# Feed-forward tiles laid out anew in SBUF, relu and square on ScalarE, Strassen-Winograd products in another order, last weights loaded in pairs

## The chip, the cores and the metric

The kernel runs on one core of a Trainium2 chip. Five engines work side by side, each on its own queue of instructions, in order: TensorE (PE, with its weight loads shown apart as PEld), VectorE (DVE), ScalarE (ACT), GpSimd (POOL) and SyncE (SP), which issues the DMAs here. Engines wait for each other on semaphores. The metric is the time of one execution on the device, in microseconds (us), as the median of the runs shown; less is better.

## The reference

One layer of a streaming encoder, for 512 prompt tokens and 64 sample tokens together (T = 576 columns), width 1024. Token mixing (a gated delta rule and a differential attention), a cross attention over a memory, and a feed-forward block, each added to the residual:

```python
h = x + concat([oa, ob]) @ w_out
h = h + mem_attn(rmsnorm(h, ln_mem_q), mem_k, mem_v, w_mem_q, w_mem_o)
hn = rmsnorm(h, ln_ffn)
h = h + square(relu(hn @ w_ff1)) @ w_ff2      # w_ff1 1024 x 4096, w_ff2 4096 x 1024
y = rmsnorm(h, ln_final)
```

All is float32. The change touches the feed-forward block and the step ahead of it.

## The kernel before

Activations lie transposed, features on the 128 partitions and tokens along the free axis, in blocks of 128 features (m = 0 to 7 for width 1024). A float32 product is made of three products of a rounded type (F32R): each operand is split into a high part, `A.copy` on ACT, and a low part, `V.tensor_tensor(... subtract)` on DVE, and PE adds high x high, high x low and low x high in PSUM.

**Order of the work.** The program is written in the order of the computation, and a planner makes from it the queue of each engine: among the instructions that it holds ready it takes the one that is earliest in the program, and `tc.high_priority()` raises what stands under it. A tile has a tag, and a tag has so many slots in its pool; an instruction that writes a new tile needs a free slot. At run time each queue is strictly in order, so an instruction that waits holds up all behind it on its engine, DMA issues on SP among them.

**Pools.** The stages up to the memory attention and `w_mem_o` use the pools `sp` (small tiles: B1, B0, kd, vb, p0, an, p1, X and so on, in this order of bytes) and `wp` (weights: `raw`, `wh`, `wl`). `work.close()` gives up both, and the pool `fp` of the feed-forward takes the same bytes, with waits tile by tile. Its tags lie in the order in which the program first names them: f1, rB, r1, s12, s34, a1h, a1l, w12h, w12l, a2h, a2l, w34h, w34l, keep, c, r2, w2h, w2l, tm.

**Ahead of the feed-forward.** For m in the order 0, 4, 1, 5, 2, 6, 3, 7, `project` multiplies with `w_mem_o`, `add_residual` adds to the residual `hT`, and `combine(m)` (L1220 to L1243) prepares the operands of a Strassen-Winograd product: the scaled activations are cut into upper and lower features (m < 4 or not) and first and second half of the tokens (N0, N1, 288 columns each), and the sums that the seven products need are split into B1, B2, T12 and T34. All sums are made in `combine(m)` for m of 4 and more. Then the squares are summed over the features by PE (`ones` and `accq`, bank `ba`), for the norm that is multiplied in later (rB).

**The first product.** `ff1_pair(p)` (L1281), p = 0 to 15, makes 256 of the 4096 hidden features. Two DMAs bring 512 KB of `w_ff1` each into r1 (two slots); DVE makes the weight sums s12 and s34 (L1293 to L1298), `split` makes a1, w12, a2 and w34 (L1270, L1271; one slot each). Then come seven products of 12 matmuls with 288 columns. Their sums stand in PSUM banks x (g0), y (gs), z (g1) and w (ba); `keep` copies a bank on ACT, `put` adds two parts on DVE (L1336), takes relu and square at once on DVE (L1337), and splits the result (L1341 on ACT, L1342 on DVE).

**The second product.** Groups of two pairs: with g = 1 to 7, the pairs 2g and 2g + 1 stand at m = 0 and m = 4, and for each m `weights2` brings 256 KB of `w_ff2` for group g - 1 into r2 (three slots), `project` multiplies, and `add_group` adds to the sum of the groups on DVE (L1372, L1374). Pairs 0 and 1 stand alone ahead, with `row_broadcast` (two ba banks) behind them. In the last group `last_weights` (L1380) brings the weights of group 7 for two m at each m of 4 and more, through r2, and splits them into the bytes of T34 and T12, which the last pair's products read. `last_block` then adds group 7 for each m, first half of the tokens, then second, and the final norm and the output follow.

PSUM has eight banks: pr (three), ba (two), g0, g1 and gs.

Of the kernel before, what the change touches and what calls it, by code (L numbers as in the profile page):

```python
# [37 lines left out]
def hybrid_layer_kernel(  # L38
# [1176 lines left out]
    T12, T34 = ([u[:, j].rearrange("p k (i t) -> p i k t", i=2) for j in range(2)] for u in (pair(2, F32R), pair(3, F32R)))  # L1215
    B1 = [cp.tile([P, 2, T], F32R, tag=f"qz{i}", name=nm("B1")).rearrange("p j (k t) -> p j k t", k=2) for i in range(2)]

    scaled = {}

    def combine(m):  # L1220


        scaled[m] = x = small("kd" if m < 4 else "aT", [P, T])
        A.activation(x, hT[m // 4][:, m % 4, :], AF.Identity, scale=gcol[:, G_FF + m : G_FF + m + 1])
        k = m % 4
        if m < 4:
            hi, lo = (B1[k // 2][:, j, k % 2, :] for j in range(2))
            A.copy(hi, x[:, N0])
            V.tensor_tensor(lo, x[:, N0], hi.bitcast(F32), ALU.subtract)
            return  # L1230
        top = scaled[k]
        t12, t34 = small("p0", [P, 2, NH]), small("an", [P, 2, NH])
        V.tensor_tensor(t12[:, 0], top[:, N1], top[:, N0], ALU.subtract)
        V.tensor_tensor(t34[:, 0], x[:, N1], top[:, N1], ALU.subtract)
        V.tensor_tensor(t12[:, 1], x[:, N1], t12[:, 0], ALU.subtract)
        V.tensor_tensor(t34[:, 1], x[:, N0], t12[:, 1], ALU.subtract)
        for (hi, lo), src in (
            ((T12[j][:, :, k, :] for j in range(2)), t12),
            ((B2[:, j, k, :] for j in range(2)), x),
            ((T34[j][:, :, k, :] for j in range(2)), t34),  # L1240
        ):
            A.copy(hi, src)
            V.tensor_tensor(lo, src, hi.bitcast(F32), ALU.subtract)  # L1243

    for m in (0, 4, 1, 5, 2, 6, 3, 7):
        project(weights(w_mem_o[0], m * P), mo, add_residual(m, True))
# [8 lines left out]
    work.close()  # L1255
    fp = ctx.enter_context(tc.tile_pool(name="fp", bufs=1, reuse_waits="tile"))

    def ft(tag, shape, bufs, dt=F32):
        return fp.tile(shape, dt, tag=tag, name=nm(tag), bufs=bufs)

    temps = lambda n: ft("tm", [P, 320], 2)[:, :n]
    odd = lambda: ft("f1", [P, 2, 4, T], 1, F32R)
    f1 = odd()
    rB = ft("rB", [P, T], 1)

# [15 lines left out]
    def ff1_pair(p, sx):  # L1281


        raw = []
        for i in range(2):
            raw.append(ft("r1", [P, 4, 2 * P], 2))
            src = w_ff1[0, 512 * i : 512 * i + 512, 2 * P * p : 2 * P * (p + 1)]
            nc.sync.dma_start(raw[i], src.rearrange("(k p) n -> p k n", p=P))
        A11, A21 = raw[0][:, :, :P], raw[0][:, :, P:]
        A12, A22 = raw[1][:, :, :P], raw[1][:, :, P:]  # L1290
        s12, s34 = (ft(tag, [P, 2, 4, P], 1) for tag in ("s12", "s34"))
        with tc.high_priority():
            V.tensor_tensor(s12[:, 0], A21, A22, ALU.add)  # L1293
            V.tensor_tensor(s12[:, 1], s12[:, 0], A11, ALU.subtract)
        a11, ws12 = split(A11, "a1", 1), split(s12, "w12", 1)
        with tc.high_priority():
            V.tensor_tensor(s34[:, 1], A12, s12[:, 1], ALU.subtract)
            V.tensor_tensor(s34[:, 0], A11, A21, ALU.subtract)  # L1298
        a2, ws34 = split(raw[1], "a2", 1), split(s34, "w34", 1)

        def block(w, c):
            return [x[:, :, c * P : (c + 1) * P] for x in w]

        def of(x, n):
            return lambda j, k: x[j][:, n, k, :]

        def half(u, n):
            return lambda j, k: u[:, j, k, n]

        operands = {  # L1310
            1: (a11, lambda j, k: B1[k // 2][:, j, k % 2, :]),
            2: (block(a2, 0), half(B2, N0)),
            3: ([x[:, 1] for x in ws34], half(B2, N1)),
            4: (block(a2, 1), of(T34, 1)),
            5: ([x[:, 0] for x in ws12], of(T12, 0)),
            6: ([x[:, 1] for x in ws12], of(T12, 1)),
            7: ([x[:, 0] for x in ws34], of(T34, 0)),
        }

        def product(i, b, start):  # L1320
            w, x = operands[i]
            for k in range(4):
                for j, (jw, jx) in enumerate(((0, 0), (0, 1), (1, 0))):
                    mm(
                        b[:, :NH], w[jw][:, k, :], x(jx, k),
                        start=start and k == j == 0, stop=k == 3 and j == 2, skip_group_check=True,
                    )

        def keep(b):
            x = ft("keep", [P, NH], 4)  # L1330
            A.copy(x, b[:, :NH])  # L1331
            return x

        def put(i, n, b, more):
            c = ft("c", [P, NH], 3)
            V.tensor_tensor(c, b, more, ALU.add)  # L1336
            V.scalar_tensor_tensor(c, c, 0.0, c, ALU.max, ALU.mult)  # L1337
            if p >= 2 * (NG - 1):
                V.tensor_tensor(c, c, rB[:, n], ALU.mult)
            hi, lo = (sx[:, j, 2 * (p % 2) + i, n] for j in range(2))  # L1340
            A.copy(hi, c)  # L1341
            V.tensor_tensor(lo, c, hi.bitcast(F32), ALU.subtract)  # L1342

        x, y, z, w = bank("g0"), bank("gs"), bank("g1"), bank("ba")
        product(1, x, True)
        s1 = keep(x)
        product(5, z, True)
        s5 = keep(z)
        product(2, y, True)
        put(0, N0, y[:, :NH], s1)  # L1350
        product(6, x, False)
        s2 = keep(x)
        product(3, z, False)
        put(0, N1, z[:, :NH], s2)
        product(7, x, False)
        s3 = keep(x)
        put(1, N1, s3, s5)
        product(4, w, True)
        put(1, N0, w[:, :NH], s3)

    accu = [None]

# [17 lines left out]
    def last_weights(m):  # L1380
        if m == 0:
            wlast.extend(pair(i, F32R) for i in (3, 2))
        hi, lo = (view(u, m // 4, 16, P)[:, 4 * (m % 4) : 4 * (m % 4) + 4] for u in wlast)
        raw = ft("r2", [P, 4, P], 3)
        nc.sync.dma_start(raw, w_ff2[0, (NG - 1) * 512 :, m * P : (m + 1) * P].rearrange("(k p) n -> p k n", p=P))
        A.copy(hi, raw)
        V.tensor_tensor(lo, raw, hi.bitcast(F32), ALU.subtract)

    def last_block(m, s, a0, n, alone=None):
        hi, lo = (view(u, m // 4, 16, P)[:, 4 * (m % 4) : 4 * (m % 4) + 4] for u in wlast)  # L1390
# [49 lines left out]
    for g in range(1, NG):  # L1440
        nxt = (f1 if g == 1 else odd()) if g % 2 else pair(5, F32R)
        for m in range(KT):
            if m % 4 == 0:
                ff1_pair(2 * g + m // 4, nxt)
            project(weights2(w_ff2[0, (g - 1) * 512 : g * 512, :], m * P), (pend,), add_group(g - 1, m), kt=4)
            if g == NG - 1:
                am, hm = accu[0][m // 4][:, m % 4, :], hT[m // 4][:, m % 4, :]
                V.tensor_tensor(am, am, rB, ALU.mult)
                V.tensor_tensor(hm, hm, am, ALU.add)
                if m >= 4:  # L1450
                    last_weights(2 * m - 8)
                    last_weights(2 * m - 7)
        pend = nxt
    pend = (pend,)

# [52 lines left out]
```

## Time and profile before

| | |
|---|---|
| median of 3 runs | 1036.83 us (1036.8 to 1037.14) |
| the profiled execution | 1037.32 us, its span 1035.6 us |
| PE busy | 1001.3 us, 97% of the span, 6630 matmuls |
| DVE, ACT busy | 733.2 us (71%), 488.5 us (47%) |
| DMA | 89.98 MB, mean 87 GB/s |
| mean granted PE clock | 0.991 |

The span is the time from the first to the last instruction of the profiled execution. Times in rows of the trace count from its start. A row of the timeline has the start, the duration, engine, line, operation, the output and input by the program's names, shapes and count, and in brackets how long the engine had been idle and what ended that. In tables of stretches a bracket holds the number of instructions. `SPq` is SP's queue; a wait `A <- B: total, times, longest` is time that A spent until B ended. All matmuls go through the helper in L107 and all transposes through L113, so tiles tell the stages apart.

### The profile page before, as it was taken

The numbers are of one execution on the slowest core, as the hardware profiler recorded it, in microseconds if no ns is written. First come the engines' busy times: TensorE is split into PE (matmuls) and PEld (weight loads), VectorE is DVE, ScalarE is ACT, GpSimd is POOL, SyncE is SP. The second block draws the span as 40 slices with busy tenths as digits, with TensorE's granted clock in tenths as the row PEclk, the third lists the DMA queues.
The fourth block names the chain that finished last, engine by engine and source line by source line (L and its number), as shares of the span: only waits on it lengthen the run. The fifth ranks groups of instructions, "written<-read, shape, count | busy, mean of one in ns | idle before, by whom it ended". The sixth has DMA issues, their size and how long they took to land.

```text
span 1035.6 us, 17242 instructions
## 1 busy us (share of the span) xinstructions
PE 1001.3 (97%) x6630; PEld 921.2 (89%) x6630; DVE 733.2 (71%) x1591; ACT 488.5 (47%) x1024; POOL 56.4 (5%) x123
## 2 busy tenths in 40 slices
PE   9999999999999999999999987999999999999986
PEld 7989899998888877999997986999999999999976
DVE  6576784776666676565665777966777777778883
ACT  6654664333465665444453554554333333343344
POOL 3431110100000000000000000000000000000000
PEclk9999999999999999999999997999999999999999
DMA  7432310100321455524111206232323232222122
GB/s 205 137 103 81 115 56 26 38 21 22 103 72 60 132 170 183 157 83 122 42 48 35 62 1 181 84 92 85 102 89 91 84 92 83 82 82 62 41 62 92
DMA packets 123365, 89.98 MB, mean 87 GB/s; under 512 B 5570, under 2 KB 114240, under 8 KB 122772
## 3 DMA queue, kind: packets, MB, share of 16 engines
q1 hardware_dynamic: 122916, 88.24, 28.7%
q8 instruction: 52, 0.85, 0.3%
q10 hardware_dynamic: 368, 0.66, 0.2%
q14 instruction: 29, 0.24, 0.1%
HBM read 79.14 MB, written 9.74 MB: 86 GB/s over the span
## 4 chain that ended last, share of the span: by engine, by line
PE 79%; DVE 6%; issue 3%; DMA 3%; ACT 3%; POOL 2%; POOLq 0%; ACTq 0%; SPq 0%; DVEq 0%
PE pr L107 46%; PE g L107 19%; PE gs L107 7%; DMA r<-in_w_ff_dram 3%; PE ba L113 2%; PE ba L107 2%; PE g L113 2%; DVE wl L162 0%; ACT w12h L1270 0%; DMA out_dram<-S 0%; POOL tg L208 0%; DVE p L457 0%; DVE a2l L1271 0%; DVE c L1336 0%; DVE c L1337 0%
## 5 line engine op out<-in xcount | busy, mean ns | idle before, releaser
L107 PE MATMUL pr<-u,wh 128*128 128x320 f32 (+2 forms) x1240 | 328.5, 342 | 1.8 <-DVE p L323 1.0
L107 PE MATMUL pr<-u,wl 128*128 128x256 f32 (+1 forms) x816 | 228.1, 303 | 0.0
L107 PEld LDWEIGHTS pr<-u,wh 128*128 128x128 f32 x1240 | 211.6, 188 | 18.1 <-DVE p L323 1.3
L107 PEld LDWEIGHTS pr<-u,wl 128*128 128x128 f32 x816 | 149.4, 188 | 3.8 <-issue 0.7
L162 DVE TENSOR_TENSOR wl<-raw,wh 128x1024 fp32r<-128x1024 f32 x65 | 79.5, 1224 | 36.6 <-ACT wh L161 36.1
L107 PE MATMUL pr<-u,w2h 128*128 128x320 f32 (+1 forms) x384 | 98.7, 340 | 5.5 <-ACT w2h L1270 3.8
L161 ACT CAST wh<-raw 128x1024 fp32r<-128x1024 f32 x65 | 68.2, 1049 | 60.5 <-PE pr L107 54.8
L1270 ACT CAST w2h<-r 128x512 fp32r<-128x512 f32 x56 | 34.7, 621 | 121.8 <-PE pr L107 102.6
L107 PE MATMUL pr<-f,w2h 128*128 128x320 f32 (+1 forms) x288 | 74.7, 340 | 0.3 <-DVE u L1374 0.2
L107 PEld LDWEIGHTS pr<-u,w2h 128*128 128x128 f32 x384 | 64.9, 188 | 10.9 <-ACT w2h L1270 4.4
L107 PE MATMUL pr<-u,w2l 128*128 128x256 f32 (+1 forms) x256 | 65.2, 295 | 0.0
L1372 DVE TENSOR_TENSOR u<-u,pr 128x256 f32<-128x256 f32 x96 | 42.2, 451 | 20.7 <-PE pr L107 20.5
L107 PEld LDWEIGHTS pr<-f,w2h 128*128 128x128 f32 x288 | 48.6, 188 | 4.1 <-issue 1.3
L107 PE MATMUL g<-u,w12h 128*128 128x288 f32 x256 | 52.2, 296 | 0.0
L107 PE MATMUL g<-u,w34h 128*128 128x288 f32 x256 | 51.7, 296 | 0.2 <-ACT keep L1331 0.2
L107 PE MATMUL pr<-f,w2l 128*128 128x256 f32 (+1 forms) x192 | 48.8, 294 | 0.0
L107 PEld LDWEIGHTS pr<-u,w2l 128*128 128x128 f32 x256 | 46.8, 188 | 1.5 <-DVE w2l L1271 0.2
L1271 DVE TENSOR_TENSOR w2l<-r,w2h 128x512 fp32r<-128x512 f32 x56 | 38.6, 690 | 8.4 <-ACT w2h L1270 8.3
L208 POOL TENSOR_TENSOR tiny<-tiny,nhalf 128x1 f32<-128x1 f32 (+4 forms) x10 | 8.3, 826 | 642.4 <-DVE tiny L1431 550.4
L107 PEld LDWEIGHTS g<-u,w12h 128*128 128x128 f32 x256 | 41.8, 189 | 0.5
L107 PEld LDWEIGHTS g<-u,w34h 128*128 128x128 f32 x256 | 41.0, 188 | 0.6 <-ACT keep L1331 0.6
L107 PE MATMUL pr<-wh,u 128*128 128x512 f32 x128 | 41.4, 402 | 0.0
(444 smaller groups left out, 2185.7 us busy)
## 6 DMA issues: line engine op xcount, KB each, us to landing
r<-in_w_ff_dram SPq DMA_DIRECT2D x32, 512.0 KB
r<-in_w_ff_dram SPq DMA_DIRECT2D x64, 256.0 KB
raw<-in_w_in_dram SPq DMA_DIRECT2D x28, 512.0 KB
raw<-in_w_mem_k_dram SPq DMA_DIRECT2D x8, 512.0 KB
raw<-in_w_mem_v_dram SPq DMA_DIRECT2D x8, 512.0 KB
raw<-in_w_out_dram SPq DMA_DIRECT2D x8, 512.0 KB
raw<-in_w_mem_q_dram SPq DMA_DIRECT2D x8, 512.0 KB
raw<-in_w_mem_o_dram SPq DMA_DIRECT2D x8, 512.0 KB
```

The costliest lines, as they stand in the source:

```text
L107: i = nc.tensor.matmul(out, lhsT, rhs, start=start, stop=stop, skip_group_check=skip_group_check)
L113: i = nc.tensor.transpose(out, in_, ident[:n, :n])
L161: A.copy(wh, raw)
L162: V.tensor_tensor(wl, raw, wh.bitcast(F32), ALU.subtract)
L208: G.tensor_tensor(out, in_, bc(nhalf[: in_.shape[0], 0:1], list(in_.shape)), ALU.pow)
L1270: A.copy(wh, src)
L1271: V.tensor_tensor(wl, src, wh.bitcast(F32), ALU.subtract)
L1372: V.tensor_tensor(am, am, b, ALU.add)
```

## The change

1. `fp` names its tags in another order, through a list of tiles made ahead of use (`laid`): r1 now has the first bytes, then keep, s12, r2, w2h, s34, a1h, a1l, w12h, w12l, a2h, a2l, w34h, rB, c, tm, w34l, f1, w2l. Sizes and numbers of slots stay.
2. `combine(m)` for m < 4 also makes the first T12 sum and its split; for m of 4 and more the second T12 sum is split alone, then B2, then T34.
3. In `put`, relu and square are two activations on ACT in place of one operation on DVE. The last `put` takes its sum straight from the bank, with no add on DVE.
4. The products come in the order 1, 5, 6, 2, 7, 3, 4 in place of 1, 5, 2, 6, 3, 7, 4. x is a ba bank in place of g0 and takes products 1, 6, 7 and 4 one upon the other; before, product 4 had a bank of its own.
5. `last_weights` loads two m with one DMA of 512 KB through r1, and splits them with one cast and one subtraction at high priority.

```diff
@@ combine
-    scaled = {}
+    scaled, steps = {}, {}
+
+    def halves_to(hi, lo, src):
+        A.copy(hi, src)
+        V.tensor_tensor(lo, src, hi.bitcast(F32), ALU.subtract)
...
         if m < 4:
-            hi, lo = (B1[k // 2][:, j, k % 2, :] for j in range(2))
-            A.copy(hi, x[:, N0])
-            V.tensor_tensor(lo, x[:, N0], hi.bitcast(F32), ALU.subtract)
+            halves_to(*(B1[k // 2][:, j, k % 2, :] for j in range(2)), x[:, N0])
+            steps[k] = t12 = small("p0", [P, 2, NH])
+            V.tensor_tensor(t12[:, 0], x[:, N1], x[:, N0], ALU.subtract)
+            halves_to(*(T12[j][:, 0, k, :] for j in range(2)), t12[:, 0])
             return
-        top = scaled[k]
-        t12, t34 = small("p0", [P, 2, NH]), small("an", [P, 2, NH])
-        V.tensor_tensor(t12[:, 0], top[:, N1], top[:, N0], ALU.subtract)
+        top, t12, t34 = scaled[k], steps[k], small("an", [P, 2, NH])
+        V.tensor_tensor(t12[:, 1], x[:, N1], t12[:, 0], ALU.subtract)
+        halves_to(*(T12[j][:, 1, k, :] for j in range(2)), t12[:, 1])
+        halves_to(*(B2[:, j, k, :] for j in range(2)), x)
         V.tensor_tensor(t34[:, 0], x[:, N1], top[:, N1], ALU.subtract)
-        V.tensor_tensor(t12[:, 1], x[:, N1], t12[:, 0], ALU.subtract)
         V.tensor_tensor(t34[:, 1], x[:, N0], t12[:, 1], ALU.subtract)
-        for (hi, lo), src in (
-            ((T12[j][:, :, k, :] for j in range(2)), t12),
-            ((B2[:, j, k, :] for j in range(2)), x),
-            ((T34[j][:, :, k, :] for j in range(2)), t34),
-        ):
-            A.copy(hi, src)
-            V.tensor_tensor(lo, src, hi.bitcast(F32), ALU.subtract)
+        halves_to(*(T34[j][:, :, k, :] for j in range(2)), t34)
@@ the pool fp
+    laid = {}
     def ft(tag, shape, bufs, dt=F32):
+        if tag in laid:
+            return laid.pop(tag)
         return fp.tile(shape, dt, tag=tag, name=nm(tag), bufs=bufs)
...
+    for tag, shape, bufs, dt in (
+        ("r1", [P, 4, 2 * P], 2, F32), ("keep", [P, NH], 4, F32), ("s12", wide_, 1, F32),
+        ("r2", block_, 3, F32), ("w2h", block_, 3, F32R), ("s34", wide_, 1, F32),
+        ("a1h", block_, 1, F32R), ("a1l", block_, 1, F32R), ("w12h", wide_, 1, F32R), ("w12l", wide_, 1, F32R),
+        ("a2h", [P, 4, 2 * P], 1, F32R), ("a2l", [P, 4, 2 * P], 1, F32R), ("w34h", wide_, 1, F32R),
+        ("rB", [P, T], 1, F32), ("c", [P, NH], 3, F32), ("tm", [P, 320], 2, F32), ("w34l", wide_, 1, F32R),
+        ("f1", [P, 2, 4, T], 1, F32R), ("w2l", block_, 3, F32R),
+    ):
+        laid[tag] = fp.tile(shape, dt, tag=tag, name=nm(tag), bufs=bufs)
@@ ff1_pair
         def put(i, n, b, more):
             c = ft("c", [P, NH], 3)
-            V.tensor_tensor(c, b, more, ALU.add)
-            V.scalar_tensor_tensor(c, c, 0.0, c, ALU.max, ALU.mult)
+            if more is None:
+                A.activation(c, b, AF.Relu)
+            else:
+                V.tensor_tensor(c, b, more, ALU.add)
+                A.activation(c, c, AF.Relu)
+            A.activation(c, c, AF.Square)
...
-        x, y, z, w = bank("g0"), bank("gs"), bank("g1"), bank("ba")
+        x, y, z = bank("ba"), bank("gs"), bank("g1")
         product(1, x, True)
         s1 = keep(x)
         product(5, z, True)
         s5 = keep(z)
+        product(6, x, False)
+        s2 = keep(x)
         product(2, y, True)
         put(0, N0, y[:, :NH], s1)
-        product(6, x, False)
-        s2 = keep(x)
+        product(7, x, False)
+        s3 = keep(x)
         product(3, z, False)
         put(0, N1, z[:, :NH], s2)
-        product(7, x, False)
-        s3 = keep(x)
         put(1, N1, s3, s5)
-        product(4, w, True)
-        put(1, N0, w[:, :NH], s3)
+        product(4, x, False)
+        put(1, N0, x[:, :NH], None)
@@ last_weights
-        hi, lo = (view(u, m // 4, 16, P)[:, 4 * (m % 4) : 4 * (m % 4) + 4] for u in wlast)
-        raw = ft("r2", [P, 4, P], 3)
-        nc.sync.dma_start(raw, w_ff2[0, (NG - 1) * 512 :, m * P : (m + 1) * P].rearrange("(k p) n -> p k n", p=P))
-        A.copy(hi, raw)
-        V.tensor_tensor(lo, raw, hi.bitcast(F32), ALU.subtract)
+        hi, lo = (
+            view(u, m // 4, 16, P)[:, 4 * (m % 4) : 4 * (m % 4) + 8].rearrange("p (i k) n -> p i k n", i=2) for u in wlast
+        )
+        raw = ft("r1", [P, 4, 2 * P], 2)
+        src = w_ff2[0, (NG - 1) * 512 :, m * P : (m + 2) * P]
+        nc.sync.dma_start(raw, src.rearrange("(k p) n -> p k n", p=P))
+        src = raw.rearrange("p k (i n) -> p i k n", i=2)
+        with tc.high_priority():
+            A.copy(hi, src)
+            V.tensor_tensor(lo, src, hi.bitcast(F32), ALU.subtract)
...
                     last_weights(2 * m - 8)
-                    last_weights(2 * m - 7)
```

More of the change, by code (lines that the diff above doesn't have):

```diff
@@ L1262, in hybrid_layer_kernel @@
     odd = lambda: ft("f1", [P, 2, 4, T], 1, F32R)
+    block_, wide_ = [P, 4, P], [P, 2, 4, P]
+    for tag, shape, bufs, dt in (
[7 more added lines that the diff above has]
+        laid[tag] = fp.tile(shape, dt, tag=tag, name=nm(tag), bufs=bufs)
     f1 = odd()
```

## The prediction

> **What bounds the kernel now.** I read the page's engine row and slices first, then the stretches around the two places where PE is not full, then the rows in time there, and last what SP waited for.
>
> ```profile
> PE 1001.3 (97%) x6630; PEld 921.2 (89%) x6630; DVE 733.2 (71%) x1591; ACT 488.5 (47%) x1024; POOL 56.4 (5%) x123
> PEclk9999999999999999999999997999999999999999
> ```
>
> PE bounds the program as a whole, so only idle PE time and slow PE clock can be won. One slice, two thirds in, has both. Stretches (columns: PE, PEld, DVE, ACT, POOL busy, granted clock, DMA share, GB/s):
>
> ```profile
> 616.00:618.00 2.00, 0.73 (x8) 0.65 (x7) 0.98 (x2) 1.36 (x3) 0.00 (x0) 1.00 0.00 0
> 618.00:622.00 4.00, 0.72 (x5) 0.63 (x4) 3.24 (x8) 1.79 (x3) 0.00 (x0) 0.51 0.00 0
> 622.00:626.70 4.70, 0.00 (x0) 0.00 (x0) 0.79 (x2) 0.60 (x1) 0.00 (x0) 0.50 0.71 222
> 626.70:631.60 4.90, 4.83 (x19) 4.61 (x20) 4.68 (x8) 3.99 (x7) 0.00 (x0) 0.50 0.87 233
> 640.50:643.00 2.50, 0.76 (x4) 0.41 (x4) 2.50 (x3) 2.49 (x4) 0.00 (x0) 1.00 0.79 240
> 643.00:654.60 11.60, 11.42 (x85) 11.19 (x86) 11.01 (x23) 5.47 (x12) 0.00 (x0) 1.00 0.29 92
> 654.60:985.00 330.40, 329.96 (x2265) 318.36 (x2264) 259.54 (x497) 128.80 (x241) 0.00 (x0) 1.00 0.28 82
> 985.00:996.60 11.60, 7.76 (x46) 6.63 (x45) 10.15 (x21) 3.72 (x6) 0.00 (x0) 1.00 0.47 136
> ```
>
> From 654.6 to 985 PE lacks 0.44 us: nothing done to DVE or ACT there can gain. The feed-forward's entry (616 to 643) and its end (985 to 996.6) remain. The entry in time, with what SP waited for:
>
> ```profile
> SPq L1288 <- DVE u L1243: 35.1, 1, 35.1
> ...
> 575.87 11.22 SPq L157 DMA_DIRECT2D raw<-in_w_mem_o_dram  x3
> 622.27 0.92 SPq L1288 DMA_DIRECT2D r<-in_w_ff_dram  x2
> ...
> 617.66 1.06 PE L107 MATMUL ba<-ones,accq 128*128 128x1 f32 x6 [1.27 <-DVE accq L1110]
> ...
> 620.73 0.67 ACT L1242 CAST u<-an 128x576 fp32r<-128x576 f32 x1 [0.37 <-DVE an L1236]
> ...
> 621.43 0.76 DVE L1243 TENSOR_TENSOR u<-an,u 128x576 fp32r<-128x576 f32 x1
> ...
> 626.10 0.62 ACT L1270 CAST a1h<-r 128x512 fp32r<-128x512 f32 x1 [4.70 <-DMA r<-in_w_ff_dram]
> 626.10 0.69 DVE L1298 TENSOR_TENSOR s<-r 128x512 f32<-128x512 f32 x1 [3.91 <-DMA r<-in_w_ff_dram]
> 626.75 0.69 DVE L1271 TENSOR_TENSOR a1l<-r,a1h 128x512 fp32r<-128x512 f32 x1
> 626.77 0.85 PE L107 MATMUL g<-B,a1h 128*128 128x288 f32 x2 [8.05 <-ACT a1h L1270]
> ```
>
> SP is done with w_mem_o's issues at 587.09, then stands 35.1 us before the first w_ff1 load, because that load's bytes lie under `an`, whose last reader (L1243) ends at 622.19. Data, cast and first product follow in series. PE also runs at half clock until 631.6.
>
> **The layout.** Counted from the shapes, the old pools' region begins with B1 and B0 (bytes 0 to 8,192 per partition); p0 lies at 16,896 to 22,016 and `an` at 22,016 to 27,136. Before, r1 lies at 20,736 to 28,928. After, r1 takes 0 to 8,192, whose last readers are the memory attention's products:
>
> ```profile
> L107 PEld LDWEIGHTS g<-an,B x8: 191/192/193, 547.9 to 571.4; 128*128 128x128 f32 x8
> ```
>
> So both w_ff1 loads of the first pair can go at 587 instead of 622.27 and are in long before they are wanted. The casts are another matter. In ACT's and DVE's queues of before, everything of the new pool stands behind the last combine (ACT 620.73, DVE 621.43, above), and I take it that this stays, since the planner lays out the new pool only when the old one's users are placed. The last combine itself shortens little: six DVE operations as before, one of them half as long. I take its end at 621.9 (0.3 earlier), a1h then runs from 621.4 to 622.0, and PE starts at 622.0 instead of 626.77: **gain 4.8**. Bounds: nothing, and 626.77 - 615.9 - 1.1 for the norm's products = 9.8 if the casts move ahead of the combine.
>
> The third matmul needs a1l. DVE runs L1298 and then a1l, 0.6 apart and 0.69 long: 623.2, which is 1.2 after the start where before it was 0.7: **loss 0.5**. The half clock lasted 4.9 us from the start; the idle stretch ahead of it shrinks from 8.1 to some 3.3 us, but the clock had fallen at 618 already. I leave it: 0 (bounds 0 and 2.4, half of 4.9). [...]
>
> **The second pair and SP's queue.** Before, PE stood 1.74 of the 2.5 us to 643 with the second pair's weights late:
>
> ```profile
> 630.84 5.08 DMA r<-in_w_ff_dram
> ...
> 636.04 0.69 DVE L1293 TENSOR_TENSOR s<-r,r 128x512 f32<-128x512 f32 x1 [1.79 <-DMA r<-in_w_ff_dram]
> ...
> 642.03 0.50 PE L107 MATMUL pr<-u,w2h 128*128 128x512 f32 x1 [1.50 <-DVE u L1342]
> ...
> 654.57 1.06 PE L107 MATMUL ba<-ident,tiny 128*128 128x128 f32 x8
> ```
>
> These loads wait for r1, so for the first pair's DVE work, which now starts 4.2 us earlier without waiting for data. The three w_ff2 loads that stand ahead of them on SP wait too: r2 now covers p0 and the first of `an`, so they go at about 620.5 to 622 instead of 623.2 to 625.3, and what is behind them is not held up further, as r1 comes free only at 624. DVE has less to do here as well (next part). Against it, product 4 had its own bank and filled PE while w12l was missing; now it adds to x behind product 7 and can't. I take **0.7 of the 1.74** (bounds -1 and 1.74). So the second pair ends at 654.57 - 5.0 = 649.6.
>
> **Relu and square.** Per pair four DVE operations of L1337 go, and one of the four adds of L1336 (put(1, N0) reads the finished sum from x); ACT gets four relus and four squares and loses one keep.
>
> ```profile
> L1337 DVE SCALAR_TENSOR_TENSOR c<-c 128x288 f32<-128x288 f32 x64 | 29.1, 456 | 1.0
> L1331 ACT COPY keep<-g 128x288 f32<-128x288 f32 x61 | 23.9, 392 | 6.8 <-PE g L107 6.8
> L1341 ACT CAST f<-c 128x288 fp32r<-128x288 f32 x32 | 13.8, 433 | 34.8 <-DVE c L1337 25.1 <-DVE c L1339 9.5
> L696 ACT ACT_TABLE_LOAD  x3: 1283/1283/1283, 125.8 to 186.1; - x3
> ```
>
> Over 16 pairs: DVE -64 x 0.456 - 16 x 0.456 = -36 us; ACT +128 x 0.392 to 0.433 - 16 x 0.392 = +44 to +49 us, and its idle time from 654.6 to 985 is 202 us. No trace has a Relu; a table load of 1.283 at each change would add 128 x 1.283 = 164 us to ACT and fill it. I take none: the run's last load is the one at 186.1, and Exp, Square, copies and casts alternate behind it. [...] In the stage itself DVE's relief is worth nothing.
>
> **The order 1 5 6 2 7 3 4.** Product 7 adds to x after keep(s2), product 4 after keep(s3), each with one product between. Before, only product 7 had so little room:
>
> ```profile
> 778.37 1.58 PE gs L107 x12
> ...
> 781.45 1.05 ACT L1270 CAST w12h<-s 128x1024 fp32r<-128x1024 f32 x1
> 782.41 0.39 ACT L1331 COPY keep<-g 128x288 f32<-128x288 f32 x1
> ...
> PE g L107 <- ACT keep L1331: 0.2, 1, 0.2
> ```
>
> A product gives 1.58 us; w12h and the keep behind it end 1.35 us after w12h's start. That fits, and cost 0.2 us in 16 pairs. After, relu, square and cast of a put share the window. I take **a loss of 0.6**; bounds 0 and one ACT operation of 0.4 at each of 32 places, 12.8.
>
> x also holds one of the two ba banks for a whole pair; the next pair takes the other. row_broadcast wants both once, between pairs; in the 0.6.
>
> **combine.** A T12 cast and its subtraction become two halves each, four times: ACT +4 x (2 x 0.43 - 0.67), DVE +4 x (2 x 0.46 - 0.76), 1.4 us together, spread under w_mem_o's products, where PE is full; if uncovered, those 1.4.
>
> **The end.** Before, the last weights shared r2's three slots with the stream that feeds PE:
>
> ```profile
> 984.43 0.37 SPq L1276 DMA_DIRECT2D r<-in_w_ff_dram  x1
> 986.76 1.60 SPq L1385 DMA_DIRECT2D r<-in_w_ff_dram  x2
> 988.76 0.37 SPq L1276 DMA_DIRECT2D r<-in_w_ff_dram  x1
> ...
> 987.39 0.62 ACT L1270 CAST w2h<-r 128x512 fp32r<-128x512 f32 x1 [3.30 <-DMA r<-in_w_ff_dram]
> ...
> 988.06 0.80 PE L107 MATMUL pr<-u,w2h 128*128 128x512 f32 x3 [2.82 <-ACT w2h L1270]
> 992.71 0.79 PE L107 MATMUL pr<-u,w2h 128*128 128x512 f32 x3 [1.01 <-ACT w2h L1270]
> ```
>
> After, four loads of 512 KB go to r1, idle once the last pair is split; two of them fit ahead of time. So PE's 2.82 + 1.01 = 3.83 us go. The splits become four of 1.05 on ACT and 1.22 on DVE instead of eight of 0.62 and 0.69, raised in priority, and must still wait for product 4, the last reader of those bytes. DVE is next: 10.15 of 11.6 us busy there, and PE's banks wait for its adds. I give back 0.8: **gain 3.0** (bounds 1 and 3.83).
>
> **Sum.** 4.8 - 0.5 + 0.7 - 0.6 + 3.0 = 7.4. The profiled execution took 1037.32 (span 1035.6 and 1.7 around it): 1029.9. The median of the runs is 0.5 lower, 1036.83: **1029.4**.
>
> **Rivals.**
> 1. The first pair's casts are placed ahead of the last combine. For: their data is there from 591 on (587.09 and the 3.8 us from issue to cast above), they are of high priority, and ACT has time. Against: the queue order above. Then PE starts right behind the norm and the half clock hardly bites: 9.8 + 2.4 + 0.7 - 0.6 + 3.0 = 15.3, so 1021.5.
> 2. The start is given back: the second pair's loads stay behind w_ff2's and PE waits for them as it did, or DVE, busy 11.01 of 11.6 us before 654.6, keeps the pace. 4.8 becomes 1: 1036.8 - 3.6 = 1033.2; with the end given back to DVE too, no change.
> 3. Slower: the keeps. Product 7 and 4 wait for a keep that stands behind a put's square and cast, 0.4 us, at 2 places in 16 pairs: 12.8 against 8.0 gained elsewhere: 1041.6. It decides from 0.25 us per place. For: room of only 0.23 us in the rows above. Against: PE's queue can hold w_ff2 products between, and DVE's lighter load brings puts sooner.
>
> **Chances.** Forecast 0.60 (1026 to 1033), first rival 0.14, second 0.13 (0.06 of it within 0.2%, which is 2.1 us and about what a measurement of this kernel tells from no change), third 0.13. So faster 0.81, same 0.06, slower 0.13. Range 1021 to 1037: it takes in the first two rivals and leaves out the third and the best of the first, under 2 in 10; the forecast's own is 1026 to 1033.
>
> **What would show it.** The first w_ff1 loads issued near 587; a1h right behind the last combine's cast with no wait for a DMA; PE's first product near 622 and the half clock still there; row_broadcast's products near 649.6; no wait for w2h after 985; keep waits of well under 1 us in all. Wrong would be: ACT table loads in the feed-forward, PE waiting for keep again and again, or a1h ahead of the last combine.

## The result, and the profile after

The changed kernel took 1035.14 us (median of 12 runs, 1033.1 to 1036.36), the kernel before 1037.08 us beside it (12 runs, 1035.79 to 1040.56): a ratio of 0.9975, 95% interval 0.9964 to 0.9985. That is 2.6 us gained (1.6 to 3.7) where 7.4 were forecast. The profiled execution took 1033.64 us, its span 1031.9 (before 1037.32 and 1035.6).

The entry of the feed-forward came out as drawn. First what SP issued and what PE, ACT and DVE did there (start, duration, idle before and its releaser):

```profile
586.73 1.12 SPq L1301 DMA_DIRECT2D r<-in_w_ff_dram  x2
620.49 2.40 SPq L1289 DMA_DIRECT2D r<-in_w_ff_dram  x3
...
620.44 0.67 ACT L1221 CAST u<-an 128x576 fp32r<-128x576 f32 x1 [1.34 <-DVE an L1241]
621.02 0.61 ACT L1283 CAST a1h<-r 128x512 fp32r<-128x512 f32 x1
...
621.69 0.85 PE L107 MATMUL ba<-B,a1h 128*128 128x288 f32 x2 [3.62 <-ACT a1h L1283]
623.16 0.61 PE L107 MATMUL ba<-B,a1l 128*128 128x288 f32 x1 [0.63 <-DVE a1l L1284]
636.62 0.53 PE L107 MATMUL ba<-u,a2h 128*128 128x288 f32 x2 [1.00 <-ACT keep L1344]
...
649.92 0.60 PE L107 MATMUL ba<-ident,tiny 128*128 128x128 f32 x4
```

The first w_ff1 loads go at 586.73 instead of 622.27, the a1h cast stands directly behind the last combine's cast with no DMA to wait for, and PE starts at 621.69 instead of 626.77. `row_broadcast`'s products behind the second pair stand at 649.92 (forecast 649.6).

The stretches (columns as in the prediction: PE, PEld, DVE, ACT, POOL busy, granted clock, DMA share, GB/s; the number in brackets counts instructions) show where the rest is missing. The kernel before:

```profile
600.00:660.00 60.00, 48.77 (x326) 46.84 (x326) 46.95 (x87) 29.56 (x52) 0.00 (x0) 0.89 0.31 92
660.00:972.00 312.00, 311.56 (x2134) 300.38 (x2133) 243.31 (x464) 120.53 (x223) 0.00 (x0) 1.00 0.29 85
972.00:1000.00 28.00, 24.16 (x157) 22.24 (x156) 24.47 (x50) 9.27 (x18) 0.00 (x0) 1.00 0.23 66
```

The changed kernel:

```profile
600.00:660.00 60.00, 53.45 (x354) 50.70 (x353) 46.86 (x84) 37.60 (x74) 0.00 (x0) 0.91 0.28 82
660.00:972.00 312.00, 310.47 (x2129) 298.99 (x2128) 213.72 (x394) 156.66 (x327) 0.00 (x0) 1.00 0.29 86
972.00:1000.00 28.00, 24.09 (x151) 21.91 (x151) 23.66 (x47) 12.24 (x25) 0.00 (x0) 1.00 0.12 38
```

At the entry PE is busy 4.68 us more. In the middle stage it is busy 1.09 us less, although DVE was relieved of 29.6 us. At the end PE lacks 3.91 us of 28, as before (3.84). The reason for the last is in PE's and DVE's rows of the changed kernel:

```profile
981.67 0.55 PE L107 MATMUL pr<-u,w2h 128*128 128x320 f32 x2 [1.70 <-DVE u L1389]
987.29 0.54 PE L107 MATMUL pr<-u,w2h 128*128 128x320 f32 x2 [2.21 <-DVE u L1391]
...
976.82 2.36 DVE L1409 TENSOR_TENSOR u<-r,u 128x1024 fp32r<-128x1024 f32 x2 [0.45 <-ACT u L1408]
980.80 0.81 DVE L1389 TENSOR_TENSOR u<-u,pr 128x256 f32<-128x256 f32 x2
982.72 1.22 DVE L1409 TENSOR_TENSOR u<-r,u 128x1024 fp32r<-128x1024 f32 x1
984.92 1.23 DVE L1409 TENSOR_TENSOR u<-r,u 128x1024 fp32r<-128x1024 f32 x1 [0.30 <-ACT u L1408]
986.73 0.42 DVE L1391 TENSOR_TENSOR u<-u,pr 128x256 f32<-128x256 f32 x1
```

PE no longer waits for w2h. It waits 1.70 + 2.21 = 3.91 us for the additions of `add_group` (L1389, L1391) that empty its pr banks, and on DVE these stand behind the big subtractions of the last weights (L1409), which the change raised in priority; between the first two of those and L1389 four smaller operations, 1.7 us in all, stand as well. One wait was exchanged for another of the same size.

### The profile page after: what moved, and what is told of

Its sections match the earlier page's. It is cut to its first block, busy times and chain, and to the rows that moved or that the text cites. A ratio compares the mean times of both kernels' runs of the same rounds, so it can differ in the third digit from the quotient of the medians.

```text
span 1031.9 us, 17262 instructions
## 1 busy us (share of the span) xinstructions
PE 1001.4 (97%) x6630; PEld 920.4 (89%) x6630; DVE 701.0 (68%) x1511; ACT 534.9 (52%) x1152; POOL 56.8 (6%) x123
## 4 chain that ended last, share of the span: by engine, by line
PE 77%; DVE 8%; DMA 4%; issue 3%; ACT 3%; POOL 2%; POOLq 0%; ACTq 0%; DVEq 0%; SPq 0%
PE pr L107 42%; PE g L107 14%; PE ba L107 9%; PE gs L107 8%; DMA r<-in_w_ff_dram 3%; PE ba L113 2%; PE g L113 2%; DVE w34l L1284 1%; DVE a2l L1284 1%; ACT w34h L1283 1%; DVE s L1307 1%; DVE s L1306 0%; DVE w2l L1284 0%; DVE wl L162 0%; DVE s L1310 0%
## 5 line engine op out<-in xcount | busy, mean ns | idle before, releaser
L1389 DVE TENSOR_TENSOR u<-u,pr 128x256 f32<-128x256 f32 x96 | 40.5, 451 | 10.6 <-PE pr L107 10.2
L1284 DVE TENSOR_TENSOR w12l<-s,w12h 128x1024 fp32r<-128x1024 f32 x16 | 19.6, 1225 | 35.7 <-ACT w12h L1283 35.7
L107 PEld LDWEIGHTS pr<-f,w2l 128*128 128x128 f32 x192 | 35.1, 188 | 1.1
L1092 DVE TENSOR_TENSOR u<-u,pr 128x256 f32<-128x256 f32 (+1 forms) x48 | 21.6, 453 | 19.9 <-PE pr L107 19.8
L457 DVE SCALAR_TENSOR_TENSOR p<-p,gcol,p 128x579 f32<-128x579 f32 x33 | 27.1, 822 | 9.0 <-ACT p L455 8.6
```

Source lines behind the costliest of these rows:

```text
L107: i = nc.tensor.matmul(out, lhsT, rhs, start=start, stop=stop, skip_group_check=skip_group_check)
L457: V.scalar_tensor_tensor(yv[:, :n], cb[:, i : i + n], cwt[:, m, i : i + 1], yv[:, :n], ALU.mult, ALU.add)
L1092: V.tensor_tensor(hm, hm, b, ALU.add)
L1284: V.tensor_tensor(wl, src, wh.bitcast(F32), ALU.subtract)
L1389: V.tensor_tensor(am, am, b, ALU.add)
```

## The experiments

All times are compared with the kernel before on the same chip; "gain" is (1 - ratio) x 1037 us, with its 95% interval. The last three columns come from the same stretches as above: idle PE from 600 to 660, matmuls in the 312 us of the middle stage (one is 312 / 2134 = 0.146 us), and idle PE from 972 to 1000. They are of one profiled execution each, and have two limits. Four kernels that do the same in the middle stage (before, layout, pairs with and without priority) count 2134 to 2143, so a difference of under ten matmuls says nothing, and between two orders of the products the count depends on which products fall into the 312 us. And idle time leaves out the clock: in four of the profiles (before + pairs with priority, before + relu and square on ScalarE, changed with them on DVE, changed with the old order) the granted clock from 972 to 1000 is 0.94, where it is 1.00 in the others, so that PE lost up to another 1.7 us there (0.06 x 28).

| kernel | median us | ratio | gain us | idle entry | matmuls middle | idle end |
|---|---|---|---|---|---|---|
| before | | 1 | 0 | 11.2 | 2134 | 3.8 |
| changed | 1035.14 | 0.9975 | 2.6 (1.6 to 3.7) | 6.5 | 2129 | 3.9 |
| before + layout | 1033.05 | 0.9955 | 4.7 (3.2 to 6.1) | 8.1 | 2143 | 3.9 |
| before + pairs, with priority | 1038.92 | 1.0007 | -0.7 (-1.9 to 0.5) | 11.5 | 2134 | 3.8 |
| before + pairs, no priority | 1033.89 | 0.9958 | 4.4 (3.1 to 5.7) | 11.3 | 2139 | 0.8 |
| before + relu, square on ScalarE | 1040.08 | 1.0017 | -1.8 (-2.7 to -0.8) | 10.0 | 2105 | 2.6 |
| the same, subtraction on GpSimd | 1044.56 | 1.0056 | -5.8 (-7.3 to -4.4) | 11.5 | 2091 | 3.2 |
| changed, no priority | 1032.41 | 0.9943 | 5.9 (4.4 to 7.4) | 6.5 | 2125 | 0.9 |
| changed, relu, square on DVE | 1032.77 | 0.9948 | 5.4 (4.0 to 6.8) | 7.5 | 2151 | 2.2 |
| changed, old order of products | 1036.54 | 0.9982 | 1.9 (0.8 to 2.9) | 6.9 | 2112 | 3.9 |
| changed, old last weights | 1036.88 | 0.9983 | 1.8 (0.8 to 2.7) | 6.8 | 2122 | 4.6 |
| changed, no priority, relu on DVE | 1029.21 | 0.9914 | 8.9 (7.7 to 10.3) | 8.3 | 2148 | 0.8 |
| the same, early pool | 1026.87 | 0.9890 | 11.4 (10.0 to 13.0) | 1.1 | 2150 | 0.8 |
| the same, first pair held back | 1028.44 | 0.9898 | 10.6 (9.1 to 11.9) | 1.7 | 2151 | 0.8 |

The theory after the result was: the layout gives what was forecast; the last weights' priority hands the end's gain back; and relu and square on ScalarE cost something or nothing, which was open.

**The layout alone.** The kernel before with the new `laid` list and nothing else.

> The kernel before with the new byte order of the feed-forward tiles alone. Theory: the entry's gain comes from the layout; the first product starts near 622 instead of 626.8, the second pair ends some 4 us earlier, nothing else moves: 1033.0 (1032 to 1034). Rival: DVE, with relu and square still on it, sets the pace of the entry, and the early start is given back before the second pair ends: 1035.5 or more.

It gained 4.7 us, more than the whole change, and PE's first product stood at 622.04, 4.7 us earlier than before. The theory held by the time and the start. But some of the start was given back, as the rival had it: before the second pair's products PE waited 2.53 us for DVE, which was 1.50 before, and `row_broadcast`'s products stood at 651.38, only 3.2 us earlier (649.92 in the changed kernel).

```profile
638.85 0.50 PE L107 MATMUL pr<-u,w2h 128*128 128x512 f32 x1 [2.53 <-DVE u L1356]
```

Another 1.05 us of the difference between the two profiled executions lies in the middle stage, which this edit doesn't touch (last part of this section).

**The last weights in pairs alone**, on the kernel before: `last_weights` as in the diff, called once for two blocks.

> The kernel before with the last weights loaded in pairs of blocks through r1, at high priority, alone. Theory: the 3.8 us that PE waited for w2h go and come back as waits of PE for DVE's adds that free the pr banks: 1037 (1036 to 1038). Rival, as I had forecast: 3 us are gained and one engine less in the way: 1034.

No gain, as the theory had it. Its PE and DVE rows at the end:

```profile
985.91 0.57 PE L107 MATMUL pr<-u,w2h 128*128 128x320 f32 x2 [1.31 <-DVE u L1372]
991.86 0.87 PE L107 MATMUL pr<-u,w2h 128*128 128x320 f32 x2 [2.50 <-DVE u L1374]
...
981.43 2.35 DVE L1392 TENSOR_TENSOR u<-r,u 128x1024 fp32r<-128x1024 f32 x2
985.04 0.81 DVE L1372 TENSOR_TENSOR u<-u,pr 128x256 f32<-128x256 f32 x2
```

1.31 + 2.50 = 3.81 us of waits for the additions took the place of 3.83 us for w2h, without any other part of the change.

**The same pairs at normal priority**, on the kernel before:

```
-        with tc.high_priority():
-            A.copy(hi, src)
-            V.tensor_tensor(lo, src, hi.bitcast(F32), ALU.subtract)
+        A.copy(hi, src)
+        V.tensor_tensor(lo, src, hi.bitcast(F32), ALU.subtract)
```

> The kernel before with the last weights in pairs of blocks through the doubled tiles, at normal priority, nothing else changed. With priority this was measured at 1.0007 of before. Theory (the pairs do take away the 3.8 us for which PE waits for w2h, and the priority of their subtractions puts the same time back on the additions that free PE's banks): 2.5 to 3.5 us faster than before. Rival (the order of the pairs is worth nothing by itself, and priority costs only together with the other parts): within 1 us of before.

It gained 4.4 us, and PE's idle time at the end fell from 3.8 to 0.8. In its rows the subtractions are spread singly between the additions, and PE waits 0.18 and 0.47 us:

```profile
990.70 0.53 PE L107 MATMUL pr<-u,w2h 128*128 128x320 f32 x2 [0.18 <-DVE u L1374]
997.76 2.59 PE L107 MATMUL pr<-f,u 128*128 128x512 f32 x13 [0.47 <-DVE u L1094]
...
981.03 1.22 DVE L1391 TENSOR_TENSOR u<-r,u 128x1024 fp32r<-128x1024 f32 x1
982.91 0.81 DVE L1372 TENSOR_TENSOR u<-u,pr 128x256 f32<-128x256 f32 x2
```

These two kernels differ in the priority alone, and by 5 us. In the profiles 3.0 us of that is idle time at the end. The kernel with the priority also lost 1.7 us to the clock (0.06 x 28; the clock is the column before the last two), as 3.4 us at half clock would, and its rows put that right behind its wait of 2.50 us: two matmuls with 320 columns take 0.73 us at 992.80 and 993.60, against 0.46 at 997.08.

```profile
972.00:1000.00 28.00, 24.19 (x150) 22.76 (x149) 23.51 (x45) 7.35 (x12) 0.00 (x0) 0.94 0.13 39
```

So the pairs do remove the waits for w2h, and the priority put them back as waits for the additions.

**The changed kernel without that priority** (the same edit on it).

> The changed kernel with the last weights' splits at normal priority; nothing else differs. Theory: the two high-priority subtractions of 1.22 us, twice, stand ahead of the adds that free the pr banks; without the priority PE's waits of 1.7 and 2.2 us at 980 to 987 fall to under 1 in all: 3 us faster than the changed kernel, 1032. Rival: DVE has more to do there than time, and the wait only moves to the last blocks: within 1 us of the changed kernel.

5.9 us against before, some 3.3 more than the change, with the end's idle time at 0.9: the theory held.

**The changed kernel with the old `last_weights`**, one block at a time through r2, at normal priority as before.

> The changed kernel with the last weights loaded block by block as before, through the third tile of 128 columns, at normal priority. Theory (in the changed kernel the waits for w2h were replaced by waits for DVE's additions of the same size, 3.9 us for 3.8): the waits for w2h return, and the time stays within 1 us of the changed kernel, 1034 to 1036. Rival (the priority alone costs, and single blocks at normal priority have no wait left with the new layout): 2 to 3 us faster, as without priority, 1032 to 1033.

The theory held: the waits for w2h are back, 4.6 us at two places (PE's waits from 972 to 1000). The time is 0.8 us over the changed kernel by the ratios, within their intervals.

```profile
PE pr L107 <- ACT w2h L1283: 4.6, 2, 2.3
```

**Relu and square back on DVE**, in the changed kernel:

```
             if more is None:
-                A.activation(c, b, AF.Relu)
+                A.copy(c, b)
             else:
                 V.tensor_tensor(c, b, more, ALU.add)
-                A.activation(c, c, AF.Relu)
-            A.activation(c, c, AF.Square)
+            V.scalar_tensor_tensor(c, c, 0.0, c, ALU.max, ALU.mult)
```

> The changed kernel with relu and square as one operation on DVE again (the last put of a pair copies its bank on ACT first). Theory: the relief of DVE is worth something only where DVE is short, at the entry and the end: 0.5 to 2 us slower than the changed kernel. Rival: ACT's added relus and squares cost the 1.2 us that the stage in between lost: 1 us faster.

The theory of that time fell: the kernel became faster, 5.4 us against before, not slower. Over the changed kernel it gained 2.8 us, the rival's way and more than its 1 us. The gain shows in the middle (2151 matmuls against 2129, 3.2 us by the count), with 1.0 us lost at the entry. At the end PE was idle 2.2 us instead of 3.9, but 1.7 us went to the granted clock there (0.94 in the mean, 0.06 x 28), so this profile shows no gain at the end:

```profile
972.00:1000.00 28.00, 25.83 (x152) 23.57 (x151) 24.51 (x50) 10.17 (x19) 0.00 (x0) 0.94 0.12 38
```

**Relu and square on ScalarE alone**, on the kernel before: one line of DVE replaced by two activations.

> The kernel before with relu and square as two activations on ScalarE, nothing else changed. Theory (a DVE that must wait for ScalarE's longer chain before its own subtraction, and is in order, frees PE's banks late, whatever the order of products): 1.5 to 2.5 us slower than before. Rival (the loss seen when relu and square went back to DVE in the changed kernel belongs to the new order, with its bank copy on ScalarE): within 0.7 us of before. Rival (DVE's 30 us of relieved work show): 1 us faster or more.

1.8 us lost: the move costs, whatever the order of the products. What PE waited for in the middle stage (total us, times, longest), with the waits of DVE and of the weight loads:

```profile
PEld g L107 <- ACT keep L1331: 4.9, 13, 1.1
PE g L107 <- ACT keep L1331: 0.9, 1, 0.9
DVE w34l L1271 <- ACT w34h L1270: 20.2, 13, 1.6
DVE u L1343 <- ACT u L1342: 8.7, 6, 1.5
```

In the kernel before the same rows read

```profile
PEld g L107 <- ACT keep L1331: 0.2, 1, 0.2
DVE w34l L1271 <- ACT w34h L1270: 6.0, 12, 0.6
DVE u L1342 <- ACT u L1341: 6.0, 12, 0.5
```

ScalarE's copies of a bank (`keep`) and its weight casts come later, once in every pair. That left two readings: DVE's place in line behind the longer chain, or ScalarE itself being late.

**The subtraction behind the chain on GpSimd**, on the former kernel:

```
-            V.tensor_tensor(lo, c, hi.bitcast(F32), ALU.subtract)
+            G.tensor_tensor(lo, c, hi.bitcast(F32), ALU.subtract)
```

> The kernel before with relu and square on ScalarE, and the subtraction behind them, of the two halves of the feed-forward's input, moved from VectorE to GpSimd, which is idle in this stage. Theory (what the move of relu and square costs is VectorE's place in line: it waits up to 1.5 us for ScalarE's chain before this subtraction, with the bank-freeing additions behind it): without that subtraction VectorE waits no longer, and the cost of 1.8 us is gone, 1037 to 1039 against 1040.1 with it. Rival (ScalarE is late with its bank copies, whatever VectorE does): still 1 to 2.5 us slower than before. A third way, GpSimd's subtraction being too late for the products that read it, would show as waits of PE for GpSimd.

The theory (DVE's place in line) fell for the old order: with DVE out of that chain the loss did not go, and the waits for ScalarE's copies stayed as they were.

```profile
PEld g L107 <- ACT keep L1331: 5.3, 13, 1.2
DVE w34l L1271 <- ACT w34h L1270: 19.5, 13, 1.9
```

So ScalarE's lateness stays as the cause in the old order. The third way, PE waiting for GpSimd, showed once, 1.3 us, at the entry, where PE waited 1.5 us for DVE before. The kernel is slower still; part of that may be DVE being held up by GpSimd (last section), so its time alone doesn't settle the question, and the place of the loss does: PE loses as much at products 3 and 7 with the subtraction on GpSimd as without (last part of this section). In the new order the weight loads wait only 0.2 us for `keep`, and the waits of PE that the profile names there are seven for DVE's additions, 1.3 us in all and 0.2 us at the longest; which operation of ScalarE makes those late was not tried.

**The old order of the products**, in the changed kernel (1 5 2 6 3 7 4 through four banks as before, relu and square on ScalarE).

> The changed kernel with the products of a pair in their former order and banks (1 and 4 through one bank each, every output quarter an addition of a kept bank); relu and square stay on ScalarE. The prediction put the new order at 0.6 us lost, with bounds of 0 and 12.8 us. Theory (the order is worth nothing, the loss in the stage comes from relu and square on ScalarE): within 1 us of the changed kernel, 1034 to 1036, and the wait of PE's pr products for DVE's u of the adds stays near 1.3 us in the stage. Rival (the order costs: two more copies of banks on ScalarE stand in the chain): 1.5 to 3 us faster than the changed kernel. Rival (the order gains, by one addition less a pair on DVE): 1.5 to 3 us slower.

0.7 us slower than the changed kernel by the ratios, with both intervals about 1 us either way. That the order is worth nothing by the time can't be told from its being worth a microsecond. The counts of the middle stage (2129 against 2112) can't tell either, since the orders differ; over the same work there is no difference (last part of this section).

**Both parts taken back**, priority and relu:

> The changed kernel with two parts taken back together: the splits of the last weights at normal priority, and relu and square on DVE. Alone these gained 2.7 and 2.4 us. Theory (two separate costs, one at the end, one in the middle stage): they add, 1029.5 to 1030.5. Rival (both undo the same waits of PE for DVE's bank-freeing adds): 1032 to 1033, no better than either.

8.9 us gained. The two add, as the theory had it: 3.3 and 2.8 us over the changed kernel singly, 6.3 together.

**The early pool**, on the former kernel. The tiles that live until the last combine (kd, p0, an, zr, aT) stay in the old pool; all others go to a second pool that is closed ahead of the w_mem_o loop, and the first pair's raw and split tiles take its bytes:

```
+    early_.close()
+    fe = ctx.enter_context(tc.tile_pool(name="fe", bufs=1, side="right", reuse_waits="tile"))
     for m in (0, 4, 1, 5, 2, 6, 3, 7):
...
-        laid[tag] = fp.tile(shape, dt, tag=tag, name=nm(tag), bufs=bufs)
+        laid[tag] = (fe if tag in FE else fp).tile(shape, dt, tag=tag, name=nm(tag), bufs=bufs)
```

> The former plus one thing: the feed-forward's raw weights and split tiles lie in a pool that is free before the output projection of the memory attention, so that the first pair's loads and casts need not wait for the last combine. This is the prediction's first rival made on purpose (first casts ahead of the last combine, 8 us better). Theory (PE's empty 6 us at the entry, the half clock behind them and the waits for a1l are the price of the late tiles): PE's first feed-forward product comes within 1 us of the norm's product, and the time is 6 to 9 us under the kernel without it, 1021 to 1024. Rival (the combine is what the products wait for, or the early casts delay it): 0 to 2 us under it.

2.5 us better than without it, nearer to the rival (0 to 2) than to the theory's 6 to 9. It is the fastest kernel of the study, 11.4 us under before. PE's first product with a1h does stand 0.4 us behind the norm's first product, as the theory had it (623.64 and 623.28), but the norm's product itself stood at 615.50 without the early pool. PE is idle only 1.1 us from 600 to 660 where it was 8.3, but from 560 to 600 it is idle 6.9 us, where it was 2.8.

**The first pair's products held back**, on the former kernel: the first matmul of each of its products is kept behind the norm's product in PE's order.

> The kernel with the early pool, and the first pair's products held behind the norm's product in PE's order. In the kernel without this, a product of the first pair stood among the output projection's matmuls, before its operands were there, and PE's busy time was 1.92 us of the 5 us from 580 to 585, with a wait of 3.3 us for a subtraction on DVE. Theory (the entry's full gain was made and half of it given back at this one place): 3 to 4.5 us faster than 1026.9, 1022.5 to 1024. Rival (the early casts on ScalarE and DVE delay the output projection whatever PE's order): within 1 us of 1026.9.

Within noise of the kernel without it: the theory fell. The idle time stayed where it was, and only the instruction that waits changed:

```profile
580.00:585.00 5.00, 1.85 (x11) 1.34 (x9) 5.00 (x7) 2.21 (x3) 0.00 (x0) 1.00 0.49 154
...
586.90 0.90 PE L109 MATMUL pr<-u,wh 128*128 128x320 f32 x2 [5.05 <-DVE u L1094]
...
582.43 1.22 DVE L1290 TENSOR_TENSOR w12l<-s,w12h 128x1024 fp32r<-128x1024 f32 x1
583.93 1.21 DVE L1290 TENSOR_TENSOR w34l<-s,w34h 128x1024 fp32r<-128x1024 f32 x1
586.04 0.81 DVE L1094 TENSOR_TENSOR u<-u,pr 128x256 f32<-128x256 f32 x2
```

DVE is full from 580 to 585 with the first pair's splits, which `split` raises in priority, and the output projection's residual additions (L1094), which free PE's banks, stand behind them. It looks like the end's mechanism at another place; the first pair's splits at normal priority were not tried.

**The middle stage over the same work.** A fair measure between orders is the time from the first matmul that reads a2h in the fifth pair to that in the fifteenth, always 1640 matmuls (us, one profiled execution for each kernel):

| | relu and square on DVE | on ScalarE |
|---|---|---|
| old order | 240.65 (before), 239.60 (layout), 240.23 and 239.57 (pairs with, without priority) | 242.31 (before + relu, square on ScalarE), 241.35 (changed, old order) |
| new order | 238.36 (changed, relu on DVE), 238.33 (no priority too), 238.46 (early pool), 238.53 (held back) | 241.41 (changed), 241.59 (no priority), 241.97 (old last weights) |

In the means, ScalarE costs 1.8 us in the old order and 3.2 in the new; the new order gains 1.6 us with DVE doing relu and square, and nothing with ScalarE. Summed from each matmul's start to the next one's, ScalarE's cost stands at one place in each order. In the old it is at products 3 and 7, which read w34: 35.3 us against 31.7 to 31.8, and 35.6 with the subtraction on GpSimd (products 5 and 6, which read w12, give some of it back: 31.8 to 31.9 us against 32.4 to 33.4). In the new it is at the products with `w_ff2`, whose pr banks DVE's additions empty: 130.0 to 130.6 us against 126.7 to 126.9, with products 3 and 7 unchanged. Of the new order's 1.6 us, 1.1 stand at products 5 and 6 and 0.8 at those with `w_ff2`; why is open. The times don't settle whether the gain reaches the whole: layout and pairs at normal priority gained 4.7 and 4.4 us, and the kernel with both and the new order 8.9. The new order was not run by itself.

## Why the prediction was wrong

**The end was mis-read, and decided.** The step that failed is "I give back 0.8: gain 3.0". That the 3.83 us of waits for w2h go was right, and so was the sentence that DVE is next. The price was not: alone the step measured -0.7 us (-1.9 to 0.5) instead of +3.0. The 0.8 was a guess laid on a row that showed DVE busy 10.15 of 11.6 us, and it charged nothing for where the raised subtractions would stand. Two of them in a row are 2.36 us, and PE stood 1.70 and 2.21 us for a pr bank until the additions behind them came. Without the priority the step gave 4.4 us (3.1 to 5.7), about its upper bound of 3.83. The bounds of 1 and 3.83 left out zero, which is where it fell.

**Relu and square were put at nothing.** "In the stage itself DVE's relief is worth nothing" stands (no run shows it gaining there), but ScalarE's load was put at nothing with it, because ScalarE was idle for 202 us of that stage. The idle time is not where the work falls: alone the step cost 1.8 us (0.8 to 2.7). No table load came (the last is at 185.7 us); the durations were as taken (440 and 441 ns for relu and square on c, 402 for relu from a bank, against the 392 to 433 from other rows). A single operation on these f32 tiles takes about as long on either engine (402 to 441 ns and 456), but ScalarE needs two of them, 881 ns, where DVE does relu and square at once in 456 ns. What that cost PE was late bank copies in the old order and late additions in the new.

**The order** was put at 0.6 lost. The changed kernel waits once, 1.00 us, for a keep. The old order in its place measured 0.7 us slower, not distinguishable. Over the same work the new order is worth nothing while ScalarE does relu and square, and gains 1.6 us in ten pairs when DVE does; so the loss was not there, and PE's 0.44 us of idle time in the stage was not all that could be won. The third rival's mechanism, a product behind a late keep in every pair, did appear, at 13 places and with 4.9 us of weight-load waits, but in the old order with relu on ScalarE; in the new order these waits are 0.2 us.

**The entry** was right in the changed kernel: 4.8 - 0.5 + 0.7 = 5.0 was forecast, and the start, the a1l wait (0.63 us) and `row_broadcast`'s products behind the second pair came within 0.4 us of their places. The terms read 5.1 for the start, 0.6 lost to a1l, 0.9 gained in the second pair's waits (1.50, 0.24 and 0.18 us became one of 1.00) and 0.8 lost to a longer half clock: 4.6, against 4.65 from 654.57 to 649.92. That the layout alone measured 4.7 is partly luck: its second pair lost 1.0 instead of gaining 0.7, because DVE, with relu and square still on it, kept PE waiting 2.53 us there, and its profile ran 1.05 us faster in the middle stage. The parts measured alone, 4.7 - 0.7 - 1.8 = 2.2, agree with 2.6 for the whole within their intervals; the order and `combine` were not measured alone.

**The first rival** had its casts behind the last combine, as the forecast took it. When its condition was made on purpose it gave 2.5 us, not the 8 it was priced at. The rows point to the early splits of high priority, which delay the additions of the stage they move into; that was not tested by itself.

**The half clock** was left at 0; the profile has it 6.6 us behind the first product instead of 5.0, about 0.8 us lost (last section).

## What to carry to other kernels

When PE's banks are emptied by an engine that works in order, as by DVE here, price each raised or added operation there by its full length times the number that can stand in a row ahead of the emptying addition, and compare it with what the banks can hold; priority on work that is not late yet is paid by what is (with the pairs alone, 3.81 us of waits for the additions in place of 3.83 for w2h). Idle time of an engine in a stage says nothing of whether it is late at the moments that count (ScalarE was idle for 202 us of the stage, and relu and square on it cost 1.8): look for the operation of it that others wait for, once per round. A combination should be undone part by part even when it is faster, since here one part gave more than the whole, and taking back two others made it 8.9 us instead of 2.6.

## What the runs showed of the hardware

The half clock at the entry came in lengths of 6.82, 10.24 and 13.66 us. Stretches of half a microsecond at its two ends, in the kernel before (the clock is the column before the last two):

```profile
618.00:618.50 0.50, 0.50 (x5) 0.50 (x4) 0.00 (x0) 0.45 (x1) 0.00 (x0) 0.60 0.00 0
...
631.50:632.00 0.50, 0.50 (x4) 0.50 (x4) 0.50 (x1) 0.50 (x1) 0.00 (x0) 0.74 1.00 354
```

and in the changed kernel:

```profile
618.00:618.50 0.50, 0.07 (x1) 0.00 (x0) 0.40 (x2) 0.03 (x1) 0.00 (x0) 0.55 0.00 0
...
628.00:628.50 0.50, 0.50 (x5) 0.50 (x4) 0.50 (x2) 0.14 (x1) 0.00 (x0) 0.71 0.63 170
```

Between the two the clock is 0.50 in every such stretch, and 1.00 ahead of them and behind. A mean of 0.60 so puts the fall 0.10 us into its stretch, 0.74 the rise 0.26 us into its own: from 618.10 to 631.76, 13.66 us. The same reading gives 10.24 us after (618.05 to 628.29), and 6.82 us with the layout alone (620.46 to 627.28). These are close to 4, 3 and 2 times 3.41 us. In nine of the other profiles the half clock there lasted, by the same reading, 10.24 us (six) or 13.65 to 13.66 (three). What sets the length no row shows. The half clock behind PE's first product was 5.0 us before, 6.6 after and 5.2 with the layout alone. Half clock for 3.41 us more or less is 1.7 us of PE's time, as much as some effects here, and each of these lengths is that of one execution.

GpSimd held up VectorE. With the subtraction on GpSimd, the a2l subtraction on VectorE took 1638 ns in the mean, against 1217 to 1223 in the kernel before (first row) and 1219 in the mean with relu and square on ScalarE and the subtraction still on VectorE:

```profile
L1271 DVE TENSOR_TENSOR a2l<-r,a2h x16: 1217/1219/1223, 629.0 to 956.5; 128x1024 fp32r<-128x1024 f32 x16
...
L1271 DVE TENSOR_TENSOR a2l<-r,a2h 128x1024 fp32r<-128x1024 f32 x16 | 26.2, 1638 | 1.2 <-PE ba L107 1.2
L1343 POOL TENSOR_TENSOR u<-c,u 128x288 fp32r<-128x288 f32 x32 | 33.4, 1046 | 299.6 <-ACT u L1342 299.6
```

From 700 to 745 two a2l subtractions start, at 719.32 and 743.65, and take 1.83 us each. GpSimd's subtractions stand beside both: at 719.18 (0.89 us) and 720.47 (1.35), at 743.51 (0.89) and 744.80 (1.35). By what means they hold VectorE up no row shows. GpSimd's subtraction of 288 columns takes 1046 ns where VectorE's takes 456 (L1342 of the kernel before).
